# Key blocks of an RWKV-7 layer: one place per block for the small products, stages a whole block apart, and receptance inputs mixed from gate block 2 on

## The chip, the cores and the metric

The kernel runs on one core of one Trainium2 chip. The metric is the device time of one execution in microseconds (us); three executions of the kernel before gave a median of 1172.75 us. In the views of the profile PE is TensorE, PEld its weight loads, DVE VectorE, ACT ScalarE, POOL GpSimd and SP SyncE, which issues most of the transfers.

## The reference, cut to what matters

A sequence of 256 tokens with 2048 channels goes through one RWKV-7 layer and one sparse-attention layer, and everything is float32. Only the first part of the first layer matters here:

```python
xx = token_shift(u) - u
mixed = u[None] + xx[None] * mu[:, None, None, :]
rkvz = jnp.einsum('nbtd,nde->nbte', mixed[:4], w_rkvz)   # four 2048 x 2048 products
w_log = -jax.nn.softplus(-(w0 + jnp.tanh(xw @ w1) @ w2)) - 0.5
decay = jnp.exp(-jnp.exp(w_log.astype(jnp.float32)))
a = jax.nn.sigmoid(a0 + (xa @ a1) @ a2)
kk = heads(k * k_k).astype(jnp.float32)
kk = kk / jnp.maximum(jnp.sqrt(jnp.sum(kk * kk, axis=-1, keepdims=True)), 1e-12)
k = k * (1.0 + (a - 1.0) * k_a)
o = wkv7_scan(rh, heads(decay), kh, vh, -kk, kk * ah.astype(jnp.float32))
```

r, k, v and z are the receptance, key, value and gate projections. The scan over time is done in four chunks of 64 tokens, for which the kernel needs, per head and chunk, the product of the decayed `-kk` with the decayed keys, and the inverse of a triangular matrix built from it.

## The kernel before, in words

**Weights and inputs.** Every float32 product is made of three matmuls: high part by high part, high by low, low by high. A weight *piece* (128 x 512 numbers) is loaded by SP into a ring of 5 raw buffers (`wraw`, L177, two pieces to a buffer here), its high part is made by ACT (`whi`, L211) and its low part by DVE (`wlo`, L190), into rings of 5 buffers each. So DVE runs at most some four pieces ahead of PE. The mixed inputs (`mx`) are made per 128 channels by `mix` (L436): DVE computes `mtmp` (L433), ACT the high part (L426), DVE the low part (L427).

**The order of the projections.** v comes first, then gate block z0 (512 columns), the sixteen key blocks k0 to k15 (128 columns each, four pieces), gate blocks z1, z2 and z3 (sixteen pieces each), and then the receptance, whose products run among the steps of the scan (first line L1321). Counting the pieces from the start, k0 begins at piece 89, z1 takes pieces 153 to 168, z2 169 to 184, z3 185 to 200.

**A key block** (`phase_k`, L760) has 16 steps of three matmuls (L595 to L597). Between the steps stand small products that prepare the scan, and each hands on to DVE, ACT and POOL:

- `k_open(j)` (L678): two matmuls (L688, L689), then tanh on ACT, a running sum on DVE (`cum`, L695), exponentials on ACT, a memset on POOL (`sp`, L696) and a product on POOL (`an`, L702). It takes the next of three `sp` buffers.
- `k_square(j)` (L704), at the end of the block: ACT squares and copies the key, DVE scales it (`f`, L709).
- `k_norm(j)` (L711): the sums of squares (L715), then DVE (`sst`, L718), a power on POOL (`rnt`, L719) and a copy on ACT (`rnx`, L721).
- `k_turn(j)` (L724): transposes `rnx` (L728); DVE makes `nk` (L733) and a part of `sp` (L734), ACT another (L735), POOL the four products of `sp` (L739); SP stores `sp` (`spd`, L740).
- `k_close(j)` (L742): eight small matmuls that read `sp` (L749, each two instructions in the trace, as L688 and L689 are), two copies on ACT (`abs`, L752 and L753), three stores by SP (`abd`, L756).

In block j, after step 2, come `k_open(j)`, `k_turn(j-2)` and `k_norm(j-1)`, and after step 12 `k_close(j-2)`. `phase_z1` (L780) does the rest for the last two blocks, after steps 0, 2, 5 and 8. Half of the results of `k_close` go into a bank that `k_norm` and `k_turn` use too (`rn`).

**The inverse.** `inverse_ops(b)` (L796) inverts the triangular matrices of eight key blocks at a time, b = 0 after `k_close(7)`, b = 1 after `k_close(15)`. It loads them by SP (`invA`, L808 to L812) and then runs some 80 small operations, nearly all on DVE (L806), in chain. What of b = 1 is not yet written when the scan begins is dealt into the scan.

**What sets the order.** From k0 to z1 PE runs its instructions as the program writes them (L952). The other engines are put in order by a scheduler that works with modelled times, and then each runs its list strictly in that order: an instruction that waits holds up everything behind it on its engine. Background generators (`mixgen`, L547, and `stage_t`, L881) write the mixed inputs and the operations of the inverse among the steps, paced by pauses in modelled nanoseconds.

Of the kernel before, what the change touches and what calls it, by code (L numbers as in the profile page):

```python
# [12 lines left out]
AF = mybir.ActivationFunctionType  # L13
# [4 lines left out]
T, D, NK = 256, 2048, 16  # L18
# [50 lines left out]
HS, HSK = 300, 4  # L69
W1D, CXG = 5, 1  # L70
KPO = 3
KP, ZP = (2, 12), (0, 2, 5, 8)
AUX = {2: ("B0",), 3: ("G",), 4: ("B1",), 5: ("Y",), 7: ("A0",), 8: ("A1",), 9: ("T",)}
AUXL = {2: ("B0",), 3: ("G",), 4: ("B1",), 5: ("Y",), 8: ("T",), 9: ("A0",), 10: ("A1",)}
OPEN = (32, "G", "B0", "B1", 3, "Y", 3, "A0", 2, "A1", 8)
# [14 lines left out]
THB = 0  # L90
APOOL = 3
PRI = dict(chPE=0, chE=100, srPE=0, srE=0, skPE=0, skE=0, stE=0, atPE=1000, atE=0, cpPE=0, w=0, mx=0)
DV, DW, DK, DZ, DT, DL, DRM = 2000.0, 1000.0, 1400.0, 1200.0, 1000.0, 8000.0, 3000.0


class Sched:
# [128 lines left out]
def hybrid_kernel(ctx: ExitStack, tc: tile.TileContext, a: dict, out: bass.AP):  # L225
    nc = tc.nc
    V, S, G, PE = nc.vector, nc.scalar, nc.gpsimd, nc.tensor
# [35 lines left out]
    def accp(name="acc"):  # L263
        n = turn.get(name, 0)
        turn[name] = n + 1
        b = role[name]
        return psum.tile([128, 512], F32, name=f"bank{b[n % len(b)]}", bufs=1)
# [77 lines left out]
    phase_done = set()  # L345
# [90 lines left out]
    def mix(nm, k):  # L436
        split_into(mixed_in(nm, k), nm, k)
# [109 lines left out]
    def mixgen():  # L547
        for names in (("w", "a"), ("z",), ("k",), ("r",)):
            for k in range(NK):
                for nm in names:  # L550
                    if not ring_free(nm):
                        yield lambda: ring_free(nm)
                    if nm in "wa":
                        while ("v", k) not in mixed:
                            yield 300.0
                    mix(nm, k)
                    yield {"w": DW, "a": DW, "k": DK, "z": DZ, "r": DRM}[nm]
        phase_done.add("mixed")
# [115 lines left out]
    c3 = lambda x: x.rearrange("p (c t) -> p c t", c=NCH)  # L674
# [3 lines left out]
    def k_open(j):  # L678
        tmp = lambda name, bufs=2: kph.tile([128, T], F32, name=name, bufs=bufs)
        k = KST[j] = {}  # L680
        if j < 2:
            k["abs"] = tmp("abs")
        k["sp"] = sp = kph.tile([128, SPW], F32, name="sp", bufs=3)
        k["pp"] = pp = sp[:, 512:512 + NCH * (CH + 1)].rearrange("p (c t) -> p c t", c=NCH)
        w2t = w2[j // 2]
        sc = (j % 2) * 128
        la = accp("la")
        PE.matmul(la[:, :256], w2t[:, 0, sc:sc + 128], hw, start=True, stop=True)  # L688
        PE.matmul(la[:, 256:], w2t[:, 1, sc:sc + 128], ha, start=True, stop=True)  # L689
        sch.t += 720  # L690
        thw, tha, cum = tmp("thw"), tmp("tha"), tmp("cum")
        S.activation(thw, la[:, :256], AF.Tanh, scale=0.5, bias=W0H[:, j:j + 1])
        S.activation(tha, la[:, 256:], AF.Tanh, scale=0.5, bias=A0H[:, j:j + 1])
        S.activation(thw, thw, AF.Copy, scale=0.5, bias=0.5)
        V.tensor_tensor_scan(cum, C("rst"), thw, 0.0, op0=OP.mult, op1=OP.add)  # L695
        G.memset(pp[:, :, 0:1], 1.0)  # L696
        S.activation(pp[:, :, 1:], c3(cum), AF.Exp, scale=-DECAY)
        k["pinv"], k["an"], k["f"] = [tmp(n, 3) for n in ("pinv", "an", "f")]
        S.activation(k["pinv"], cum, AF.Exp, scale=DECAY)
        S.activation(k["an"], tha, AF.Copy, scale=-0.5, bias=-0.5)  # L700
        S.activation(k["f"], tha, AF.Identity, scale=KAH[:, j:j + 1], bias=KAM[:, j:j + 1])
        G.tensor_tensor(k["an"], k["an"], k["pinv"], op=OP.mult)  # L702
# [8 lines left out]
    def k_norm(j):  # L711
        k = KST[j]
        k["rn"] = rn = accp("rn")
        for tt in range(2):
            PE.matmul(rn[:, 256 + 2 * tt:258 + 2 * tt], k["sqk"][:, tt * 128:(tt + 1) * 128], C("bo"), start=True, stop=True)  # L715
        sch.t += 410
        sst, rnt = [kph.tile([128, 2, 2], F32, name=n, bufs=2) for n in ("sst", "rnt")]
        V.tensor_scalar(sst, rn[:, 256:260].rearrange("p (a b) -> p a b", a=2), 1e-24, None, op0=OP.max)  # L718
        G.tensor_tensor(rnt, sst, half[:, 0:4].rearrange("p (a b) -> p a b", a=2), op=OP.pow)  # L719
        k["rnx"] = kph.tile([128, T], F32, name="rnx", bufs=2)  # L720
        S.activation(k["rnx"].rearrange("p (a b n) -> p a b n", a=2, b=2),  # L721
                     rnt[:, :, :, None].to_broadcast([128, 2, 2, 64]), AF.Copy)

    def k_turn(j):  # L724
        k = KST[j]
        rn, sp, an, f, pinv = [k[n] for n in ("rn", "sp", "an", "f", "pinv")]
        for tt in range(2):
            PE.transpose(rn[:, tt * 128:(tt + 1) * 128], k["rnx"][:, tt * 128:(tt + 1) * 128], ident)  # L728
        sch.t += 215
        k["BK"] = BK = sp[:, 0:512].rearrange("p (c x t) -> p c x t", c=NCH, x=2)  # L730
        k["at"] = at = sp[:, SPW - 256:]
        nk = kph.tile([128, T], F32, name="nk", bufs=2)
        V.scalar_tensor_tensor(nk, k["ksb"], KKN[:, j:j + 1], rn[:, :256], op0=OP.mult, op1=OP.mult)  # L733
        V.tensor_tensor(c3(at), c3(nk), k["pp"][:, :, 0:CH], op=OP.mult)  # L734
        S.activation(sp[:, SPW - 512:SPW - 256], f, AF.Copy, scale=RK[:, j:j + 1])  # L735
        for x, y, o in ((f, pinv, 1), (nk, an, 0)):
            for h in range(2):
                r = slice(64 * h, 64 * h + 64)
                G.tensor_tensor(BK[r, :, h ^ o, :], c3(x)[r], c3(y)[r], op=OP.mult)  # L739
        nc.sync.dma_start(spd[j], sp)  # L740

    def k_close(j):  # L742
        k = KST.pop(j)
        ab = accp("ab")
        for c in range(NCH):
            for h in range(2):
                r, o = [slice(64 * i, 64 * i + 64) for i in (h, h ^ (c % 2))]
                pc = (ab, k["rn"])[c % 2][o, (384 if c % 2 else 0) + c // 2 * 64:]
                PE.matmul(pc[:, :64], c3(k["at"])[r, c, :], k["BK"][r, c, h, :], start=True, stop=True)  # L749
        sch.t += 500  # L750
        abs_ = k["abs"] if j < 2 else kph.tile([128, T], F32, name="abs", bufs=2)
        S.activation(abs_[:, 0:128], ab[:, 0:128], AF.Copy)  # L752
        S.activation(abs_[:, 128:256], k["rn"][:, 384:512], AF.Copy)  # L753
        for c, src, dst in ((0, 0, 0), (2, 0, 64), (2, 64, 0)):
            n = 64 if c else 128
            nc.sync.dma_start(abd[j, c:c + 2, :, dst:dst + n].rearrange("c k p s -> p (c k) s"),  # L756
                              abs_[src:src + n, 64 * c:64 * c + 128].rearrange("p (n s) -> p n s", s=32))
        a1done.add(j)

    def phase_k(j):  # L760
        if j % 2 == 0 and j + 2 < NK:
            load_pair(j // 2 + 1)
        o = accp("acc")[:, :T]
        for q in range(4):
            for s, cost in enumerate(cols_step(o, "k", q)):
                yield cost
                n = 4 * q + s
                if n == KP[0]:
                    k_open(j)
                    if j > 1:  # L770
                        k_turn(j - 2)
                    if j:
                        k_norm(j - 1)
                elif n == KP[1] and j > 1:
                    k_close(j - 2)
            if j == NK - 1:
                used.update(("k", k) for k in range(4 * q, 4 * q + 4))
        k_square(j, o)

    def phase_z1():  # L780
        turn["acc"] += 4
        ps = two()
        for k in range(NK):
            yield from rows_step(ps, "z", k, W.get(), 512)
            if k == ZP[0]:
                k_turn(NK - 2)
                k_norm(NK - 1)
            elif k == ZP[1]:
                k_close(NK - 2)
            elif k == ZP[2]:  # L790
                k_turn(NK - 1)
            elif k == ZP[3]:
                k_close(NK - 1)
        close_z(1, ps, [kph.tile([128, 512], F32, name="zth", bufs=2) for _ in range(2)], nc.sync)

    def inverse_ops(b):  # L796
# [6 lines left out]
        PE, V, S, G = Ranked(nc.tensor, "stE"), Ranked(nc.vector, "stE"), Ranked(nc.scalar, "stE"), Ranked(nc.gpsimd, "stE")  # L803

        def op(eng, n, fn, *args, pause=0.0, **kw):
            ops.append((eng, n, lambda: fn(*args, **kw), pause))  # L806
# [6 lines left out]

        flat = Tm.rearrange("p a b -> p (a b)")
        fa = A.rearrange("p a b -> p (a b)")
        op("Q", 0, load, pause=10000.0 if b else 6000.0)
        op("G" if b else "V", 1024, (G if b else V).memset, Tm, 0.0, pause=500.0)
        op("V", 32, V.memset, flat[:, 0::33], 1.0)
        op("V", 16, V.tensor_copy, flat[:, 32::66], fa[:, 32::66], pause=1000.0)
# [6 lines left out]
        for lv in (2, 4):  # L826
            n = 32 // (2 * lv)
# [1200 lines left out]
```

## Time and profile before

| | |
|---|---|
| median of three runs (lowest, highest) | 1172.75 us (1171.05, 1173.44) |
| the profiled execution's own time | 1173.38 us |
| its span, first to last instruction | 1171.5 us |
| PE busy | 1117.0 us, 95% |
| DVE busy | 874.9 us, 75% |
| ACT busy | 715.8 us, 61% |
| POOL busy | 365.9 us, 31% |
| bytes moved | 225.35 MB, mean 192 GB/s |

The profiled execution lies 0.63 us above the median, and 1.9 us of its time lie outside the span. Times in the views count from the span's start. In a row of the timeline stand the start, the duration (both us), the engine, the line, the operation and in brackets how long the engine had been idle before it and what it waited for. Rows of the grouped view hold the sum of the busy time and the mean duration in ns. In the view by windows the number in brackets counts instructions, and PEclk is the TensorE clock granted, 1.00 being full. Some matmul records are missing from a trace, so that counts can be a few short.

### The profile page before, as it was taken

Reading aid. Unit: us, or ns where it says so; the run is one execution under the profiler, and the core shown is the slowest. Engines: PE = TensorE matmul, PEld = TensorE weight load, DVE = VectorE, ACT = ScalarE, POOL = GpSimd, SP = SyncE. Lnnn points to the kernel's source line nnn. Section 1 sums busy time; section 2 is a strip of 40 time slices with the busy share of each in tenths; the row PEclk is TensorE's granted clock in tenths of the full one; section 3 lists DMA queues with packets and bytes.
Section 4 is the critical chain, followed back from the end, with each engine's and each line's share of the span. In section 5 each row is a group of like instructions: output and inputs, shape, how many; then the busy total and the mean of one; then the engine's idle time right before and its main releaser. Section 6 shows DMA issues by size and latency. Waiting matters only on the chain.

```text
span 1171.5 us, 24532 instructions
## 1 busy us (share of the span) xinstructions
PE 1117.0 (95%) x8880; PEld 948.3 (81%) x8880; DVE 874.9 (75%) x1807; ACT 715.8 (61%) x1696; POOL 365.9 (31%) x460
## 2 busy tenths in 40 slices
PE   8999989987789999899999999999999999999997
PEld 7788889976578777687778888788889989888786
DVE  6999866689855888587665878585576888988564
ACT  5667677767446455455564766575556676666553
POOL 1400046745441553555100001010233334452211
PEclk9999999999799999899999999999999999999999
DMA  6558967876698966867446867676665553748553
GB/s 221 171 182 244 255 189 214 226 202 171 192 251 233 254 174 183 235 151 215 125 154 194 254 195 238 209 252 192 171 176 148 144 141 95 190 117 273 172 184 108
DMA packets 239033, 225.35 MB, mean 192 GB/s; under 512 B 58053, under 2 KB 185333, under 8 KB 238912
## 3 DMA queue, kind: packets, MB, share of 16 engines
q1 hardware_dynamic: 233632, 217.17, 63.3%
q0 software_dynamic: 5280, 6.61, 2.3%
q8 instruction: 70, 1.15, 0.4%
q14 instruction: 51, 0.42, 0.1%
HBM read 200.48 MB, written 23.10 MB: 191 GB/s over the span
## 4 chain that ended last, share of the span: by engine, by line
PE 73%; DVE 10%; DMA 5%; POOL 5%; issue 4%; ACT 2%; SPq 0%; POOLq 0%; ACTq 0%; DVEq 0%
PE bank L577 11%; PE bank L579 11%; PE bank L576 11%; PE bank L1321 5%; PE bank L601 4%; DVE wlo L190 3%; POOL sp L739 3%; PE bank L602 2%; PE bank L1324 2%; PE bank L241 2%; PE bank L595 2%; PE bank L596 2%; PE bank L597 2%; PE pair L1343 1%; DMA spd<-sp 1%
## 5 line engine op out<-in xcount | busy, mean ns | idle before, releaser
L190 DVE TENSOR_TENSOR wlo<-wraw,whi 128x512 fp32r<-128x512 f32 (+2 forms) x616 | 448.7, 743 | 177.0 <-ACT whi L211 166.5
L211 ACT ACTIVATE whi<-wraw 128x512 fp32r<-128x512 f32 (+2 forms) x664 | 401.8, 620 | 243.3 <-PE bank L579 95.8
L577 PE MATMUL bank<-wlo,mx 128*128 128x512 f32 (+3 forms) x576 | 218.7, 381 | 5.5 <-DVE wlo L190 4.6
L579 PE MATMUL bank<-whi,mx 128*128 128x512 f32 (+3 forms) x576 | 216.9, 379 | 0.0
L576 PE MATMUL bank<-whi,mx 128*128 128x512 f32 (+3 forms) x576 | 190.9, 381 | 1.2 <-ACT whi L211 0.5
L577 PEld LDWEIGHTS bank<-wlo,mx 128*128 128x128 f32 x576 | 110.1, 191 | 24.5 <-DVE wlo L190 6.6
L576 PEld LDWEIGHTS bank<-whi,mx 128*128 128x128 f32 x576 | 109.3, 191 | 19.6 <-ACT mx L1909 1.2
L579 PEld LDWEIGHTS bank<-whi,mx 128*128 128x128 f32 x576 | 110.0, 191 | 17.0 <-POOL mx L1910 0.4
L1321 PE MATMUL bank<-mx,whi 128*128 128x512 f32 x256 | 102.7, 432 | 0.0
L190 POOL TENSOR_TENSOR wlo<-wraw,whi 128x512 fp32r<-128x512 f32 (+2 forms) x48 | 63.8, 1331 | 110.0 <-ACT whi L211 89.2
L601 PE MATMUL bank<-mx,whi 128*128 128x512 f32 x240 | 86.7, 397 | 0.0
L595 PE MATMUL bank<-mx,whi 128*128 128x256 f32 (+1 forms) x288 | 86.1, 299 | 0.3 <-ACT mx L426 0.3
L596 PE MATMUL bank<-mx,whi 128*128 128x256 f32 (+1 forms) x288 | 83.1, 289 | 0.0
L597 PE MATMUL bank<-mx,wlo 128*128 128x256 f32 (+1 forms) x288 | 83.0, 288 | 0.0
L577 PE MATMUL bank<-wlo,kvh 128*128 128x512 f32 x192 | 76.9, 401 | 0.0
L579 PE MATMUL bank<-whi,kvl 128*128 128x512 f32 x192 | 76.1, 396 | 0.0
L1324 PE MATMUL bank<-mx,wlo 128*128 128x256 f32 x256 | 71.0, 285 | 0.0
L602 PE MATMUL bank<-mx,wlo 128*128 128x256 f32 x256 | 70.5, 285 | 0.2 <-DVE wlo L190 0.2
L576 PE MATMUL bank<-whi,kvh 128*128 128x512 f32 x192 | 67.3, 395 | 0.0
L426 ACT ACTIVATE mx<-mtmp 128x256 fp32r<-128x256 f32 x96 | 38.6, 412 | 31.0 <-DVE mtmp L433 30.9
L595 PEld LDWEIGHTS bank<-mx,whi 128*128 128x128 f32 (+1 forms) x288 | 55.6, 193 | 2.3 <-ACT mx L426 0.7
L1321 PEld LDWEIGHTS bank<-mx,whi 128*128 128x128 f32 x256 | 48.2, 190 | 10.6
(344 smaller groups left out, 2326.9 us busy)
## 6 DMA issues: line engine op xcount, KB each, us to landing
wraw<-in_a_w_rkvz_dram SPq DMA_DIRECT2D x128, 512.0 KB, 5.3
wraw<-in_kv_w_dram SPq DMA_DIRECT2D x48, 512.0 KB, 4.5
wraw<-in_b_w_in_dram SPq DMA_DIRECT2D x40, 512.0 KB, 4.2
wraw<-in_a_w_o_dram SPq DMA_DIRECT2D x32, 512.0 KB, 4.6
wraw<-in_b_w_o_dram SPq DMA_DIRECT2D x32, 512.0 KB, 4.4
spd<-sp SPq DMA_DIRECT2D x16, 642.0 KB, 4.3
wraw<-in_b_w_in_dram SPq DMA_DIRECT2D x24, 384.0 KB, 3.3
spl<-spd SPq DMA_DIRECT2D x14, 642.0 KB, 6.4
```

Source lines behind the costliest of these rows:

```text
L190: eng.tensor_tensor(lv, src, hv.bitcast(F32), op=OP.subtract)
L211: self.nc.scalar.activation(hv, src, AF.Copy)
L576: PE.matmul(o, mh[:, ts], wh[:, 0, :], start=k == ends[0], stop=False)
L577: PE.matmul(o, mh[:, ts], wl[:, 0, :], start=False, stop=False)
L579: PE.matmul(o, ml[:, ts], wh[:, 0, :], start=False, stop=k == ends[1])
L595: PE.matmul(o, wh[:, s, :], mh, start=k == 0 and first, stop=False, **kw)
L596: PE.matmul(o, wh[:, s, :], ml, start=False, stop=False, **kw)
L597: PE.matmul(o, wl[:, s, :], mh, start=False, stop=k == NK - 1, **kw)
L601: PE.matmul(o, wh[:, s, :], joint[nm, k], start=k == 0, stop=False, **kw)
L602: PE.matmul(o[:, :T], wl[:, s, :], mh, start=False, stop=False, **kw)
L1321: both = lambda: PE.matmul(o, wh[:, s, :], joint["r", k], start=k == 0, stop=k == NK - 1)
L1324: PE.matmul(o[:, :T], wl[:, s, :], mixed["r", k][0], start=False, stop=False)
```

## The change

In a key block all small products now stand in one place, after step 3, in the order `k_close(j-3)`, `k_open(j)`, `k_turn(j-2)`, `k_norm(j-1)`. A block's `k_close` thus comes a whole block after its `k_turn`, where it came ten steps after it. In z1 the same order goes on after steps 0, 6 and 12. `k_close` writes to two banks of its own. The mixed inputs of the receptance are written after z1 instead of from the end of k15 on, with a shorter pause (2000 for 3000), and the pause after the load of the second inverse is shorter (8000 for 10000). The number of instructions of each kind stays.

```diff
-KP, ZP = (2, 12), (0, 2, 5, 8)
+KP, ZP = 3, (0, 6, 12)
...
-DV, DW, DK, DZ, DT, DL, DRM = 2000.0, 1000.0, 1400.0, 1200.0, 1000.0, 8000.0, 3000.0
+DV, DW, DK, DZ, DT, DL, DRM = 2000.0, 1000.0, 1400.0, 1200.0, 1000.0, 8000.0, 2000.0
...
+                    if nm == "r" and k == 0:
+                        yield lambda: "z1" in phase_done
                     mix(nm, k)
...
     def k_close(j):
         k = KST.pop(j)
-        ab = accp("ab")
+        ab, cd = accp("ab"), accp("ab")
...
-                pc = (ab, k["rn"])[c % 2][o, (384 if c % 2 else 0) + c // 2 * 64:]
-                PE.matmul(pc[:, :64], c3(k["at"])[r, c, :], k["BK"][r, c, h, :], start=True, stop=True)
+                PE.matmul((ab, cd)[c % 2][o, c // 2 * 64:c // 2 * 64 + 64], c3(k["at"])[r, c, :], k["BK"][r, c, h, :], start=True, stop=True)
...
-        S.activation(abs_[:, 128:256], k["rn"][:, 384:512], AF.Copy)
+        S.activation(abs_[:, 128:256], cd[:, 0:128], AF.Copy)
...
-                if n == KP[0]:
-                    k_open(j)
-                    if j > 1:
-                        k_turn(j - 2)
-                    if j:
-                        k_norm(j - 1)
-                elif n == KP[1] and j > 1:
-                    k_close(j - 2)
+                if n == KP:
+                    for lag, part in ((3, k_close), (0, k_open), (2, k_turn), (1, k_norm)):
+                        if j >= lag:
+                            part(j - lag)
...
-            if k == ZP[0]:
-                k_turn(NK - 2)
-                k_norm(NK - 1)
-            elif k == ZP[1]:
-                k_close(NK - 2)
-            elif k == ZP[2]:
-                k_turn(NK - 1)
-            elif k == ZP[3]:
-                k_close(NK - 1)
+            if k in ZP:
+                for lag, part in ((3, k_close), (2, k_turn), (1, k_norm)):
+                    j = NK + ZP.index(k) - lag
+                    if j < NK:
+                        part(j)
+        phase_done.add("z1")
...
-        op("Q", 0, load, pause=10000.0 if b else 6000.0)
+        op("Q", 0, load, pause=8000.0 if b else 6000.0)
```

Lines of the changed kernel differ by a few: L733 becomes L735, L739 L741, L749 L750, L806 L800.

PE, inside a key block: what stood before after step 2 (the closing products stood 30 matmuls further down, after step 12).

```order
L597 MATMUL bank_2765<-mx_1428,wlo 128x256
L688 MATMUL bank_2780<-hw,w2s 128x256
L689 MATMUL bank_2780<-ha,w2s 128x256
L728 MATMUL bank_2678<-cst,rnx 128x128 x2
L715 MATMUL bank_2810<-cst,t_2758 128x2 x2
L595 MATMUL bank_2765<-mx_1444,whi 128x256
```

PE, inside a key block of the changed kernel, after step 3:

```order
L599 MATMUL bank_2492<-mx_1444,wlo 128x256
L750 MATMUL bank_2509<-sp 64x64 x2
L750 MATMUL bank_2510<-sp 64x64 x2
L750 MATMUL bank_2509<-sp 64x64 x2
L750 MATMUL bank_2510<-sp 64x64 x2
L690 MATMUL bank_2526<-hw,w2s 128x256
L691 MATMUL bank_2526<-ha,w2s 128x256
L730 MATMUL bank_2423<-cst,rnx 128x128 x2
L717 MATMUL bank_2556<-cst,t_2485 128x2 x2
L597 MATMUL bank_2492<-mx_1467,whi 128x256
```

The closing products (L750, alternately to two banks; a row gathers several of them) now come ahead of the opening ones; the transposes and sums follow as before.

POOL, one key block, before: the memset of the next `sp` buffer stands ahead of all four products of L739.

```order
L696 MEMSET sp_3176 128x4
L739 TENSOR_TENSOR sp_3047<-f_3062,pinv_3060 64x4x64 x2
L739 TENSOR_TENSOR sp_2908<-nk_3198,an_2922 64x4x64 x2
L719 TENSOR_TENSOR rnt_3211<-sst_3210,half_108 128x4
L702 TENSOR_TENSOR an_3190<-an_3190,pinv_3189 128x256
```

POOL, one key block, in the changed kernel:

```order
L741 TENSOR_TENSOR sp_3188<-f_3203,pinv_3201 64x4x64 x2
L698 MEMSET sp_3325 128x4
L741 TENSOR_TENSOR sp_3051<-nk_3347,an_3065 64x4x64 x2
L721 TENSOR_TENSOR rnt_3360<-sst_3359,half_108 128x4
L704 TENSOR_TENSOR an_3339<-an_3339,pinv_3338 128x256
```

The memset now stands between the two pairs; the first pair belongs to the block that turns next, the second to the one that has just been turned.

DVE, end of z1 and start of z2 in the changed kernel (the first row is the 167th `wlo`; `mtmp` and `mx` are the receptance's mixed inputs, L800 the inverse):

```order
L190 TENSOR_TENSOR wlo<-wraw,whi 128x512
L427 TENSOR_TENSOR mx_4474<-mtmp,mx_4474 128x256
L433 SCALAR_TENSOR_TENSOR mtmp<-xx,prm,xn 128x256
L190 TENSOR_TENSOR wlo<-wraw,whi 128x512
L800 TENSOR_REDUCE invT<-invX 128x8x8
L190 TENSOR_TENSOR wlo<-wraw,whi 128x512
L427 TENSOR_TENSOR mx_4519<-mtmp,mx_4519 128x256
L433 SCALAR_TENSOR_TENSOR mtmp<-xx,prm,xn 128x256
L190 TENSOR_TENSOR wlo<-wraw,whi 128x512
L427 TENSOR_TENSOR mx_4541<-mtmp,mx_4541 128x256
L800 TENSOR_TENSOR invX<-invT,invM 128x512
L190 TENSOR_TENSOR wlo<-wraw,whi 128x512
```

DVE, the end of the first inverse before:

```order
L733 SCALAR_TENSOR_TENSOR nk<-ksb,par,bank_3894 128x256
L190 TENSOR_TENSOR wlo<-wraw,whi 128x512
L806 TENSOR_TENSOR invX<-invT,invM 128x1024
L190 TENSOR_TENSOR wlo<-wraw,whi 128x512
L734 TENSOR_TENSOR sp<-nk,sp 128x256
L190 TENSOR_TENSOR wlo<-wraw,whi 128x512
L806 TENSOR_REDUCE invT<-invX 128x8x8
L190 TENSOR_TENSOR wlo<-wraw,whi 128x512 x5
```

Before, the last row of the first inverse stands after the 165th `wlo`; now it stands after the 180th, and seven of its rows after the 168th. Its first row (a copy from `invA`) stood after the 134th `wlo` and stands now after the 138th. Of the sixteen `mx` rows of the receptance, all sixteen stood ahead of the 163rd `wlo`; now twelve stand ahead of the 168th, and the last after the 173rd. The first row of the second inverse stood after the 173rd and stands after the 194th.

## The prediction

> **What bounds the kernel now.** I read the view by windows first, cut where the code changes stage: the key blocks until the first inverse begins (157.6 to 237.0), the rest of them and of z1 while it runs, the end of z1, and z2 with z3 until the receptance begins at 377.4. The last three rows look at short stretches behind waits.
>
> ```profile
> core 0: us, PE busy (x) PEld busy (x) DVE busy (x) ACT busy (x) POOL busy (x), PEclk, DMA share, GB/s
> 157.60:237.00 79.40, 74.65 (x670) 70.55 (x669) 51.34 (x79) 59.02 (x155) 51.58 (x62) 0.98 0.76 208
> 237.00:316.00 79.00, 59.95 (x442) 52.92 (x441) 76.34 (x163) 47.86 (x121) 38.00 (x42) 0.91 0.64 179
> 316.00:328.20 12.20, 12.20 (x53) 9.84 (x54) 4.02 (x7) 4.62 (x9) 8.79 (x17) 0.74 0.94 309
> 328.20:377.40 49.20, 46.13 (x197) 37.71 (x196) 28.44 (x62) 25.25 (x44) 10.85 (x21) 0.97 0.90 237
> ...
> 176.00:179.00 3.00, 3.00 (x15) 2.98 (x15) 1.07 (x2) 2.20 (x7) 0.91 (x3) 0.51 0.65 182
> 301.00:304.00 3.00, 2.95 (x23) 2.41 (x24) 3.00 (x8) 1.05 (x4) 0.00 (x0) 0.63 0.79 231
> 257.60:260.60 3.00, 3.00 (x34) 2.90 (x35) 2.90 (x8) 1.94 (x6) 1.79 (x2) 1.00 0.78 219
> ```
>
> Two bounds follow each other. In the first window PE is busy for 94% and DVE for 65%: PE sets the pace, and what it loses are waits. In the second DVE is busy for 76.34 of 79.00 us and PE for 59.95: DVE sets the pace. From 328.2 on PE leads again, with DVE at 58%. The waits of PE from 150 to 380 have two rows that matter, both for the closing products:
>
> ```profile
> PE bank L749 <- POOL sp L739: 14.7, 12, 3.4
> PE bank L749 <- DVE sp L734: 9.1, 3, 5.2
> ```
>
> Their places and the edges of the stages stand in PE's timeline:
>
> ```profile
> 157.63 0.60 PE L688 MATMUL bank<-hw,w2s 96*128 96x256 f32 x2
> ...
> 165.50 0.59 PE L688 MATMUL bank<-hw,w2s 96*128 96x256 f32 x2
> ...
> 173.51 0.32 PE L749 MATMUL bank<-sp 64*64 64x64 f32 x2 [2.73 <-POOL sp L739]
> ...
> 225.39 0.75 PE L749 MATMUL bank<-sp 64*64 64x64 f32 x16
> ...
> 236.72 0.59 PE L688 MATMUL bank<-hw,w2s 96*128 96x256 f32 x2
> ...
> 256.79 0.32 PE L749 MATMUL bank<-sp 64*64 64x64 f32 x2 [1.05 <-POOL sp L739]
> ...
> 301.05 0.46 PE L749 MATMUL bank<-sp 64*64 64x64 f32 x16 [2.78 <-DVE sp L734]
> ...
> 315.19 0.33 PE L749 MATMUL bank<-sp 64*64 64x64 f32 x2 [3.40 <-POOL sp L739]
> ...
> 339.38 0.80 PE L577 MATMUL bank<-wlo,mx 128*128 128x512 f32 x1 [3.07 <-DVE wlo L190]
> ...
> 377.38 0.39 PE L1321 MATMUL bank<-mx,whi 128*128 128x512 f32 x1
> ```
>
> A block without a stall takes 157.63 to 165.50, 7.87 us. The eight from k3 (165.50) to k11 (236.72) took 71.22 where eight times 7.87 is 62.96, so 8.3 us were lost, to such waits and to the slow clock behind them (0.51 in the window at 176). DVE's timeline shows the second bound:
>
> ```profile
> 238.94 0.18 DVE L806 COPY invT<-invA 128x16 f32<-128x16 f32 x1 [5.51 <-DMA invA<-abd]
> ...
> 310.82 0.47 DVE L733 SCALAR_TENSOR_TENSOR nk<-ksb,par,bank 128x256 f32<-128x256 f32 x1
> ...
> 320.30 0.69 DVE L190 TENSOR_TENSOR wlo<-wraw,whi 128x512 fp32r<-128x512 f32 x1 [3.81 <-ACT whi L211]
> ...
> 322.87 0.69 DVE L190 TENSOR_TENSOR wlo<-wraw,whi 128x512 fp32r<-128x512 f32 x1 [1.88 <-ACT whi L211]
> ...
> 338.08 0.18 DVE L806 COPY invT<-invA 128x16 f32<-128x16 f32 x1 [5.95 <-DMA invA<-abd]
> 338.17 0.18 DVE L806 TENSOR_TENSOR invM<-invA,invT 128x32 f32<-128x32 f32 x1
> ```
>
> The first inverse begins at 238.94, after DVE had waited 5.51 us for its load. From there DVE works on, nearly without a gap, until `nk` of block 15 at 310.82. The last `wlo` of z1 (the 168th) is the row at 322.87. So z1 ends when DVE has done everything that stands between the inverse's first row and the 168th `wlo`.
>
> **The change part by part.** I count from the order of the changed kernel what stands on DVE between those two rows, and price it from the rows grouped by form of 140 to 365:
>
> ```profile
> L190 DVE TENSOR_TENSOR wlo<-wraw,whi 128x512 fp32r<-128x512 f32 x106 | 81.7, 778 | 40.8 <-ACT whi L211 39.1 <-PE bank L688 1.5
> ...
> L806 DVE TENSOR_TENSOR invX<-invT,invM 128x1024 f32<-128x1024 f32 x2 | 2.4, 1212 | 0.0
> ...
> L806 DVE TENSOR_REDUCE invT<-invX 128x64 f32<-128x512 f32 x2 | 1.3, 672 | 0.0
> ...
> L427 DVE TENSOR_TENSOR mx<-mtmp,mx 128x256 fp32r<-128x256 f32 x16 | 8.1, 514 | 0.0
> ...
> L433 DVE SCALAR_TENSOR_TENSOR mtmp<-xx,prm,xn 128x256 f32<-128x256 f32 x13 | 6.9, 540 | 0.0
> ```
>
> A row begins about 0.08 before the one ahead has ended (338.08 plus 0.18 is 338.26, the next begins at 338.17), so each is worth its duration less 0.08.
>
> *The inverse's start.* Its load reads the stores of `k_close(7)`. That ran at 225.39 in block 9, and the copy came 13.55 later. Now `k_close(7)` stands after step 3 of block 10. Block 10 would begin seven blocks after 165.50, at 220.6 if nothing stalls, and its closing products come 0.36 later; I add 0.5 for a leftover stall, which makes 221.5. With the same 13.55 the copy comes at 235.0, 3.9 us earlier. The closing products themselves no longer wait: the order puts a whole block, 7.87 us, between the turn of a block and its close, and at a distance of ten steps they waited 2.73 at 173.51 and 1.05 at 256.79. So nearly all of the 8.3 goes, but only 3.9 counts, since DVE then waits for the load. The second bank costs nothing that I can find: the two copies on ACT remain, and the banks come free a block later. Bounds: 0 if the load lands as much later, 8.3 if it waits for nothing.
>
> *Less work on DVE before z1 ends.* Four `wlo` now stand ahead of the copy (138 for 134): 4 x 0.70, the middle between 0.69 alone less 0.08 and the mean of 0.78, makes 2.8. Seven rows of the inverse stand behind the 168th `wlo`: four of 1024 elements, 4 x 1.13, and three of 512, 3 x 0.60 (0.672 rounded, less 0.08), make 6.3. Four `mx` stand behind it, 4 x 0.43 makes 1.7, and two `mtmp`, 2 x 0.46 makes 0.9. Sum: 11.7. Nothing comes in their place. The bound below is 0, if the rows wait on something else; above it is 13, at full durations.
>
> The mean `wlo` took 778 ns, against 690 in the quiet rows at 320.30 and 322.87; POOL works beside the slower ones. [...]
>
> *The waits at z1's end.* DVE waited 3.81 + 1.88 = 5.7 between `nk` of block 15 and the 168th `wlo`, because ACT and the weight ring stood behind PE, and PE behind the close at 315.19. Now the last close comes six steps after its turn, so the 5.7 go. Bounds: 0 and 5.7; I take the upper, since what is late next is `wlo` itself.
>
> *The tail.* The 168th `wlo` ended at 323.56, z1 at about 328.2, 4.6 later, as PE had to catch up at a clock of 0.74. A z piece takes 1.36, by two rows of the chain of waits:
>
> ```profile
> 348.98 0.45 PE bank L576 x2
> ...
> 350.34 0.45 PE bank L576 x2
> ```
>
> If PE has been waiting for `wlo`, the tail is 1.4 at least. I take 2.3, another 2.3 less.
>
> Sum at z1's end: 3.9 + 11.7 + 5.7 + 2.3 = 23.6 earlier.
>
> *z2 and z3.* They took 49.2 (328.2 to 377.4), of which 32 x 1.36 = 43.5 is the pace. PE waited 3.07 at 339.38, since DVE stood 5.95 at 338.08 for the second inverse's load with the next `wlo` behind it. In the changed order that first row stands after the 194th `wlo` instead of the 173rd, and its load is asked for well ahead. So the wait of 3.07 goes. But the 6.3 + 1.7 = 8.0 us of DVE work displaced from z1 falls here, at the moment when DVE has no lead: of it I charge 3.3 in place of 5.7, and z2 with z3 take 46.8: 2.4 gained. Bounds: 43.5, all hidden in DVE's idle 20.8 us, and 51.5, all in PE's way (2.3 lost).
>
> *The clock.* One gap will remain: at z1's step 0 the turn of block 14 waits for `rnx`, made only after DVE and POOL have worked off the norm. The rows at 301.05 and in its window show a gap of 2.78 and then 0.63 for 3 us: 1.1 us lost. I charge 1.0. Behind the 1.05 at 256.79, the window at 257.6 shows 1.00. [...]
>
> From 377.4 on the orders of PE, DVE and ACT agree row by row, save 60 rows of the inverse instead of 62 in the scan: nothing.
>
> In all 23.6 + 2.4 - 1.0 = 25.0. On the profiled execution's own 1173.38 that gives 1148.4; the median is 0.63 lower, and the forecast is 1172.75 - 25.0 = 1147.8.
>
> **The rivals.**
>
> *Slower: one place per block makes a loop through POOL.* Everything now turns over once a block: POOL's memset of an `sp` buffer waits for the store of its earlier contents, behind it stand the pair `nk`, `rnt`, and then ACT's `rnx`, without which the next turn holds PE, and each later matmul, up.
>
> ```profile
> L739 POOL TENSOR_TENSOR sp<-nk,an 64x256 f32<-64x256 f32 x32 | 33.9, 1058 | 14.7 <-DVE nk L733 11.9 <-DVE sst L718 0.6
> ...
> L721 ACT ACTIVATE rnx<-rnt 128x256 f32<-128x256 f32 x16 | 6.6, 414 | 15.9 <-POOL rnt L719 15.9
> ...
> L719 POOL TENSOR_TENSOR rnt<-sst,half 128x4 f32<-128x4 f32 x16 | 19.6, 1223 | 1.3
> ```
> ```profile
> 162.98 7.62 DMA spd<-sp
> ```
> ```profile
> spd<-sp SPq DMA_DIRECT2D x16, 642.0 KB, 4.3
> ```
>
> From a block's opening at T: about 0.9 for the opening products, 0.4 for the turn, 0.5 for `nk` and 2 x 1.06 for POOL's pair bring the store to T + 3.9. With the longest landing seen, 7.62, the memset comes at T + 11.5, that is 3.6 into the next block; the pair, `rnt` and `rnx` add 2.1 + 1.2 + 0.4, so `rnx` is there at 7.3, and it is needed at 7.87 + 0.7 + 0.9 = 9.4. The median landing of 4.3 leaves 5.4. It decides from landings of about 9.7 on. If each of ten blocks then lost a wait like that at 173.51 with the clock behind it, 2.73 + 3 x 0.49 = 4.2, that would be 42 lost against 25 gained: about 1190. Against it: no landing seen is so long. Chance 0.08.
>
> *Half of it.* DVE stays the bound, but its displaced rows and the receptance's mixing cost PE in z2 all that they save in z1 (z2 and z3 at 51.5, 4.7 more than forecast), and the load is as late as before (the 3.9 gone): 25.0 - 8.6 = 16.4; if the waits at z1's end stay too, 10.7. That is 1156 to 1162. For it speaks that DMA is busy for 0.90 to 0.94 of the time at the end of z1 and after. Chance 0.20.
>
> *All of it.* PE runs at its own pace throughout. Its idle time in the four windows is 4.75 + 19.05 + 0 + 3.07 = 26.9, and the clock cost, on PE's busy time, 74.65 x 0.02 + 59.95 x 0.09 + 12.20 x 0.26 + 46.13 x 0.03 = 11.5, so up to 38: 1135 to 1141. DVE's load in the second window speaks against it. Chance 0.06.
>
> *Nothing.* The receptance begins earlier, but the scan's opening then waits for what the inverses give, and the end stays. The last row of the first inverse stands only 12 `wlo` behind z1's end, with the receptance yet to come: chance 0.04, 1172.
>
> **How the numbers follow.** The forecast has 0.62, with a range of its own of 1141 to 1155 (its bounds on the start, on z2 and on the tail, each some 2 to 4 us, seldom all on one side). The range of 8 in 10 takes it in, two thirds of the half case and a little of the full one: 1139 to 1161. A measurement of this kernel can tell about 0.2%, 2.3 us, from no change. Faster by more: 0.62 + 0.20 + 0.06 = 0.88; within it: 0.04; slower: 0.08.
>
> **What would show each step right or wrong.** Right: no wait at the closing products longer than 1 us before z1; the opening of k11 at about 229; the copy at about 235 after a wait of DVE of some 3 us for its load; z1's end at about 304; the first matmul of the receptance at about 352; its distance to the end unchanged at 794. Wrong would be: the transposes of `k_turn` waiting for `rnx` in block after block; the copy's wait as long as before with PE no earlier; a `wlo` group that stays at 778 ns and more with PE waiting for it through z2; or a first receptance matmul 25 us earlier and an end that has not moved.

## The result, and the profile after

The changed kernel takes 1142.82 us (median of five runs, 1142.49 to 1144.25), the kernel before 1171.94 (five runs, 1169.30 to 1173.44): a ratio of 0.9755, 95% interval 0.974 to 0.9771, so some 29 us faster where 25 were forecast. The profiled executions have spans of 1171.5 and 1140.4, 31.1 apart; that of before lies 1.4 above the median of its five runs, that of after 0.3 below.

The view by windows of the changed kernel, cut at the same events as before (up to the first inverse's first row; from there to the end of z1; z2 with z3; the receptance and the rest), and one short stretch:

```profile
core 0: us, PE busy (x) PEld busy (x) DVE busy (x) ACT busy (x) POOL busy (x), PEclk, DMA share, GB/s
157.30:233.30 76.00, 76.00 (x708) 72.66 (x707) 52.85 (x84) 62.84 (x160) 53.22 (x65) 1.00 0.85 242
233.30:303.70 70.40, 63.08 (x455) 53.73 (x454) 69.69 (x153) 47.21 (x119) 40.32 (x44) 0.93 0.66 197
303.70:348.40 44.70, 44.46 (x196) 36.19 (x195) 36.11 (x76) 26.73 (x47) 19.11 (x32) 1.00 0.98 293
348.40:1140.40 792.00, 772.54 (x6749) 649.01 (x6747) 576.52 (x1194) 471.09 (x1133) 234.74 (x287) 0.99 0.63 185
...
277.20:283.70 6.50, 6.50 (x32) 5.00 (x33) 6.50 (x10) 2.90 (x9) 2.63 (x3) 0.50 0.65 203
```

In the first window PE is never idle and at full clock. In the second VectorE (DVE) is busy for 69.69 of 70.40 us. In the third PE is busy for 44.46 of 44.70. What PE still waits for, from 150 to 380:

```profile
PE bank L578 <- ACT ksb L710: 5.0, 1, 5.0
PE bank L717 <- ACT t L709: 1.3, 3, 0.4
PE bank L750 <- POOL sp L741: 0.7, 1, 0.7
```

The closing products waited 23.8 us before (14.7 on POOL's `sp`, 9.1 on DVE's); now 0.7. In their place one wait of 5.0 is left. Its row, and the edges of the stages, in PE's timeline:

```profile
157.31 0.59 PE L690 MATMUL bank<-hw,w2s 96*128 96x256 f32 x2
...
219.80 0.46 PE L750 MATMUL bank<-sp 64*64 64x64 f32 x16
...
236.56 0.46 PE L750 MATMUL bank<-sp 64*64 64x64 f32 x14 [0.68 <-POOL sp L741]
...
277.20 0.80 PE L578 MATMUL bank<-whi,mx 128*128 128x512 f32 x1 [4.98 <-ACT ksb L710]
...
348.39 0.39 PE L1315 MATMUL bank<-mx,whi 128*128 128x512 f32 x1
```

And in DVE's timeline the first rows of the two inverses, with the last `wlo` of z1 between them; ACT's first row on z1's result marks that stage's end:

```profile
233.32 0.19 DVE L800 COPY invT<-invA 128x16 f32<-128x16 f32 x1 [3.80 <-DMA invA<-abd]
...
300.37 0.68 DVE L190 TENSOR_TENSOR wlo<-wraw,whi 128x512 fp32r<-128x512 f32 x1
...
335.42 0.19 DVE L800 COPY invT<-invA 128x16 f32<-128x16 f32 x1 [0.43 <-DMA invA<-abd]
```
```profile
303.85 1.24 ACT L647 ACTIVATE zth<-bank 128x512 f32<-128x512 f32 x2
```

The same events in both traces (before, z1's end by that mark is 328.42):

| stage, us | before | after | gained | forecast |
|---|---|---|---|---|
| first row of the first inverse, at | 238.94 | 233.32 | 5.6 | 3.9 |
| from there to the end of z1's last `wlo` | 84.6 | 67.7 | 16.9 | 17.4 |
| from there to z1's end | 4.9 | 2.8 | 2.1 | 2.3, less 1.0 for the clock at z1's start |
| z2 and z3, to the receptance | 49.0 | 44.5 | 4.4 | 2.4 |
| receptance, scan and the rest | 794.1 | 792.0 | 2.1 | 0 |

### The profile page after: what moved, and what is told of

It is laid out like the page before. It is cut to its first block, busy times and chain, and to the rows that moved or that the text cites. A ratio compares the mean times of both kernels' runs of the same rounds, so it can differ in the third digit from the quotient of the medians.

```text
span 1140.4 us, 24521 instructions
## 1 busy us (share of the span) xinstructions
PE 1106.3 (97%) x8880; PEld 939.2 (82%) x8880; DVE 873.3 (77%) x1807; ACT 716.3 (63%) x1696; POOL 368.9 (32%) x460
## 4 chain that ended last, share of the span: by engine, by line
PE 73%; DVE 11%; DMA 6%; issue 4%; POOL 3%; ACT 2%; SPq 0%; ACTq 0%; POOLq 0%; DVEq 0%
PE bank L579 12%; PE bank L581 12%; PE bank L578 12%; PE bank L603 5%; PE bank L1315 4%; DVE wlo L190 3%; PE bank L604 3%; PE bank L241 2%; PE bank L1318 2%; PE bank L597 2%; PE bank L598 2%; PE bank L599 2%; PE pair L1337 2%; DVE mtmp L433 1%; PE pair L1339 1%
## 5 line engine op out<-in xcount | busy, mean ns | idle before, releaser
L597 PE MATMUL bank<-mx,whi 128*128 128x256 f32 (+1 forms) x288 | 83.7, 291 | 0.3 <-ACT mx L426 0.3
L598 PE MATMUL bank<-mx,whi 128*128 128x256 f32 (+1 forms) x288 | 82.1, 285 | 0.0
```

What stands on the lines that cost most here:

```text
L597: PE.matmul(o, wh[:, s, :], mh, start=k == 0 and first, stop=False, **kw)
L598: PE.matmul(o, wh[:, s, :], ml, start=False, stop=False, **kw)
```

## The experiments

The theory of the prediction: from the first inverse's first row on, what stands on DVE up to the last `wlo` of z1 sets z1's end; the places of the small products change that list, and the block between a turn and its close takes PE's waits away. Rivals: the gain comes from the receptance's inputs; or PE's waits were all, and DVE's list counts for nothing. Each kernel ran beside the kernel before on the same chip (medians there 1170.65 to 1171.6), so ratios are compared.

**The places alone, and the rest alone.** The gate and the pause of the receptance's inputs turned out to move no instruction: without them, the order of the changed kernel is the same row for row on every engine, and twelve of the sixteen mixed inputs still stand ahead of z1's last `wlo`. Only the pause of the second inverse's load moves rows. The first kernel takes all of that away, the second has only that.

```diff
-DV, DW, DK, DZ, DT, DL, DRM = 2000.0, 1000.0, 1400.0, 1200.0, 1000.0, 8000.0, 2000.0
+DV, DW, DK, DZ, DT, DL, DRM = 2000.0, 1000.0, 1400.0, 1200.0, 1000.0, 8000.0, 3000.0
...
-                    if nm == "r" and k == 0:
-                        yield lambda: "z1" in phase_done
...
-        op("Q", 0, load, pause=8000.0 if b else 6000.0)
+        op("Q", 0, load, pause=10000.0 if b else 6000.0)
```

> Only the places of the small products and the second bank are changed; the receptance's inputs and both pauses are as before. Theory (the end of z1 is set by what stands on VectorE between the first inverse's first row and the last wlo of z1, and only the places change that list): nearly the whole gain stays, 1142 to 1145 us, and the receptance begins at 348 to 350. Rival (a good part of the gain comes from the receptance inputs written later): 1155 to 1168.

> Only the receptance's inputs (written after z1, pause 2000) and the pause of the second inverse's load are changed; places and banks are as before. Theory: the rows on VectorE ahead of z1's end stand as before, so 1169 to 1173 us, no more than 3 below the kernel before, and the waits at the closing products stay. Rival: 10 or more below the kernel before.

Measured: the places alone 1147.64 us, 0.9807 (0.9785 to 0.9828); the inputs and pauses alone 1171.51 us, 1.0006 (0.9991 to 1.002). The rival is out. But the first lies above the 1142 to 1145 expected and 0.4 to 0.5% above the changed kernel (0.9755 above, 0.9772 when measured again below, where the intervals touch), and it starts the receptance at 348.9, only 0.5 later. It loses the rest in the scan. PE's timeline shows one wait there that the changed kernel lacks:

```profile
441.36 1.12 PE L1188 MATMUL pair<-cst,O 64*64 64x64 f32 x32 [2.25 <-DVE O L1176]
```

and DVE's timeline what stood ahead of `O`:

```profile
434.60 0.67 DVE L798 TENSOR_REDUCE invT<-invX 128x32 f32<-128x512 f32 x1
```

It is the last reduction of the second inverse, and on ACT, too, two copies of its result stand ahead of the rows that make `O`. In the changed kernel the reduction stands at 428.72. With the long pause, nine more rows of the second inverse on DVE (69 for 60) are left for the scan. Aligned on the same matmuls, the two traces stand 0.8 apart the other way at 431 and 3.3 this way at 463. So the pause is worth about 4 us, though alone, in the kernel before, it is worth nothing.

**A later start of the inverse, with no wait.** The closing products keep their three blocks, but stand nine steps later.

```diff
+                if n == 12 and j > 2:
+                    k_close(j - 3)
                 if n == KP:
-                    for lag, part in ((3, k_close), (0, k_open), (2, k_turn), (1, k_norm)):
+                    for lag, part in ((0, k_open), (2, k_turn), (1, k_norm)):
```

> The changed kernel, but the closing products of block j-3 stand after step 12 of block j instead of after step 3: a block and nine steps behind their turn. They still wait for nothing, but the first inverse can begin only nine steps, 3.3 us, later. Theory (VectorE's list from that first row sets z1's end): the first row comes at about 236.5 instead of 233.3, z1 ends and the receptance begins 2 to 3.5 later, 1144.5 to 1146.5 us. Rival (the gain is PE's waits at the closing products alone): the same time as the changed kernel, 1142 to 1143.5.

Measured 1143.6 us, 0.9768 (0.9748 to 0.9789): no difference from the changed kernel, as the rival had it, so this run alone does not speak against the rival. Its profiled execution, 1139.67 us, lies 3.9 below the median. The first row came where it was expected:

```profile
236.50 0.18 DVE L802 COPY invT<-invA 128x16 f32<-128x16 f32 x1 [3.43 <-DMA invA<-abd]
```

But the last `wlo` of z1 ended at 300.29, not later than the 301.05 of the changed kernel. I had priced the start and taken the list behind it as given. Counted row by row, that list took 63.8 us for 67.7: one `wlo` and four of the key blocks' rows stand ahead of the first row, where DVE has time while it waits for the load, and the inverse's rows ran 1.4 shorter, while two more `mx` and one more `mtmp` stand in the list. A start and the list behind it can't be priced apart.

**Receptance inputs really late.** Each reads a copy of the mixing factors that depends on the turn of block 15.

```diff
+    def late_mu(src):
+        m = ph1.tile([128, NK], F32, name="mur", bufs=1)
+        V.scalar_tensor_tensor(m, src, 0.0, MU[0], op0=OP.mult, op1=OP.add)
+        MUR.append(m)
...
-        mu = MU[{"r": 0, "k": 1, "v": 2, "z": 3, "w": 4, "a": 5}[nm]]
+        mu = MUR[0] if nm == "r" else MU[{"r": 0, "k": 1, "v": 2, "z": 3, "w": 4, "a": 5}[nm]]
...
+                        if part is k_turn and j == NK - 1:
+                            late_mu(KST[j]["BK"].rearrange("p a b c -> p (a b c)")[:, 0:NK])
```

> The changed kernel, but the receptance's mixed inputs really come late: each reads a copy of the mixing factors that is made from a product of block 15's turn, so none of them stands ahead of the last wlo of z1 (twelve did). The seven rows of the first inverse that stood behind z1 stand ahead of it instead, and the second inverse's first row stands after the 175th wlo. Theory: VectorE has 12 mx and as many mtmp less, 11 us, and 7 inverse rows more, 6.3, ahead of z1's end, and ScalarE's copy of block 15's key no longer stands behind a mixing (PE waited 4.98 there): z1 ends 4 to 7 earlier; z2 and z3 give back up to 5, as all mixing falls there and the second inverse's first row may wait for its load again: 1137 to 1144 us, most likely 1140. Rival (that wait and the mixing are off the path): the same as the changed kernel or slower, 1143 to 1147.

Measured 1151.88 us, 0.9834 (0.9812 to 0.9857): some 8 us slower than the changed kernel, against my expectation. PE's timeline and its view by windows:

```profile
277.55 0.79 PE L585 MATMUL bank<-whi,mx 128*128 128x512 f32 x1 [5.01 <-ACT ksb L717]
...
320.95 0.79 PE L586 MATMUL bank<-wlo,mx 128*128 128x512 f32 x1 [3.95 <-DVE wlo L190]
```
```profile
275.00:305.60 30.60, 28.05 (x153) 22.26 (x154) 28.16 (x48) 18.00 (x39) 8.78 (x11) 0.83 0.66 205
305.60:357.00 51.40, 45.99 (x190) 36.92 (x189) 36.34 (x88) 27.73 (x53) 18.64 (x35) 0.93 0.95 256
```

Two things took the gain. DVE's list up to z1's last `wlo` is as long as before the edit, 67.8 us: its twelve `mx` and eight of its eleven `mtmp` are gone from it, 10.0 us, but seven more rows of the inverse (6.0), longer small rows (1.9) and 2.4 of waits fill the place. And the second inverse's first row moved from behind the 194th `wlo` to behind the 175th, where DVE waits 5.62 for its load at 319.69 and PE behind it 3.95: the same wait that the kernel before had at 339.38. By ACT's mark z1 ends at 304.89 (the windows above are cut at 305.60), 1.0 later than in the changed kernel, and z2 and z3 take 52.1 for 44.5. The wait for `ksb` did not go either. In the changed kernel ACT waits ahead of `ksb` for two `mtmp` of DVE (2.22 and 0.45); here the mixing is gone from there, and ACT waits instead for DVE's `cum` and then 0.43 for POOL's `rnt`:

```profile
274.25 0.42 ACT L706 ACTIVATE sp<-cum 128x256 f32<-128x256 f32 x1 [1.98 <-DVE cum L704]
```

In both kernels ACT is held up there mostly by DVE, for 2.67 us and for 1.98.

**More work on DVE, in three kernels.** The low part of eight pieces is computed twice, 8 x 0.69 = 5.5 us: pieces 158 to 165, in z1, in the changed kernel and in the kernel before, and pieces 105 to 112, in key blocks 4 and 5, in the changed kernel.

```diff
         self.due.append((lv, src, hv, eng))
+        if 157 <= self.split < 165:
+            self.due.append((lv, src, hv, eng))
```

> The changed kernel with the low part of eight weight pieces in z1 (158 to 165) computed twice on VectorE: 8 x 0.69 = 5.5 us more on its list ahead of z1's end, and nothing else. The theory of the prediction (VectorE's list up to the last wlo sets z1's end): z1 ends 4.5 to 5.5 later, 1147.5 to 1148.5 us. The theory that the first experiments left standing (PE sets z1 itself, and VectorE's lateness reaches PE only through the chain of the small products): 0 to 2 more, 1143 to 1145.

> The kernel before with the same eight low parts computed twice. Both theories expect a loss here, since the wlo stand ahead of the nk and sp of the last two blocks, for which PE waits at the closing products: 3 to 7 us, 1174 to 1178. If it stays within 1 us of the kernel before, VectorE was not the bound of z1 there either, and the gain came from somewhere else.

The third kernel has 104 and 112 for 157 and 165.

> The changed kernel with the low part of eight pieces of key blocks 4 and 5 (105 to 112) computed twice: 5.5 us more on VectorE while it has a third of its time free, ahead of the first inverse. Theory (VectorE is the bound only from the first inverse's first row to the end of z1): 0 to 1 more, 1142 to 1144. Rival (any work on VectorE counts, through the clock or through the small products): 3 to 10 more.

Measured: in z1 of the changed kernel 1158.66 us, 0.99 (0.9879 to 0.9921), some 15 us more than the changed kernel; in z1 of the kernel before 1174.11 us, 1.003 (1.0019 to 1.0041), 3.5 more; in the key blocks of the changed kernel 1145.02 us, 0.9788 (0.977 to 0.9807), 1.7 more than the changed kernel beside it, with intervals that overlap, between what the theory and the rival expected and nearer to the theory (its first inverse starts 1.9 later, at 235.23). PE's waits in the first of them, and its windows of z1 and of z2 with z3:

```profile
PE bank L581 <- DVE wlo L190: 9.9, 7, 2.1
PE bank L580 <- ACT ksb L712: 5.0, 1, 5.0
```
```profile
277.00:314.30 37.30, 30.39 (x156) 22.28 (x156) 37.27 (x67) 18.19 (x43) 8.06 (x8) 0.90 0.58 174
314.30:363.70 49.40, 45.25 (x186) 35.04 (x186) 31.29 (x67) 25.25 (x45) 19.74 (x37) 0.97 0.94 261
```

The dose lands on the path in full: DVE has not a tenth of a us idle in z1, its list is 6.1 longer (73.8), and PE, which waited for no `wlo` in the changed kernel, now waits for seven. What I had not expected is the multiple: the receptance begins 15.4 later (363.76 for 348.39). PE's last matmul of z1 comes 8.6 later (312.66 for 304.06; ACT's row at 314.29, which marks the end of the window, is late here, as ACT copies a result of the inverse first), and the other 6.8 fall in z2 and z3. They are not the dose on the list alone. The edit also moved the second inverse's first row, from behind the `wlo` of piece 194 to behind that of piece 183, where DVE waits for its load and PE then 1.90 for the next `wlo`, at 338.02:

```profile
336.73 0.18 DVE L802 COPY invT<-invA 128x16 f32<-128x16 f32 x1 [3.32 <-DMA invA<-abd]
```

In the kernel before, the same dose was taken up by idle time: the waits of DVE on the way to z1's last `wlo` shrank from 5.69 to 0.68 and the list stayed at 84.6. The 3.5 that it costs there cannot be placed, since its profiled execution, which lies 1.7 below the median, reaches the receptance at 377.53 (377.38 before).

**z1 without the wait at its start.** It accumulates in banks that block 15 does not use, and its small products stand after steps 4, 9 and 14.

```diff
-KP, ZP = 3, (0, 6, 12)
+KP, ZP = 3, (4, 9, 14)
...
-        turn["acc"] += 4
```

> The changed kernel, but z1 accumulates in the two banks that block 15 does not use, and its small products stand after steps 4, 9 and 14 instead of 0, 6 and 12, so that z1 can begin while VectorE, GpSimd and ScalarE still work off the last blocks. The theory that PE is the bound of z1 and lost 4.98 us of wait at its first step and some 3 by the clock behind it: 5 to 8 us less, 1135 to 1138. The theory of the prediction (VectorE's list is the bound): no more than 1 less, 1142 to 1144.

Measured 1147.44 us, 0.9805 (0.9785 to 0.9824), slower than the changed kernel. PE's timeline and a window:

```profile
279.02 0.50 PE L579 MATMUL bank<-wlo,mx 128*128 128x512 f32 x1 [3.00 <-DVE wlo L190]
...
293.84 0.46 PE L750 MATMUL bank<-sp 64*64 64x64 f32 x16 [1.45 <-DVE sp L736]
...
352.20 0.63 PE L1314 MATMUL bank<-mx,whi 128*128 128x512 f32 x1 [2.57 <-DVE vt L649]
```
```profile
271.00:304.30 33.30, 27.41 (x169) 21.30 (x168) 33.30 (x60) 21.18 (x51) 15.88 (x16) 1.00 0.62 190
279.00:282.50 3.50, 2.86 (x11) 2.08 (x12) 3.50 (x6) 2.44 (x6) 0.74 (x1) 1.00 0.51 194
```

The wait for `ksb` is gone, the clock stays at 1.00, PE works on at z1 from 272.9, where it had stood until 277.2, and z1 ends at 304.3, no earlier than without the edit (303.85): PE now waits for DVE, 3.00 and 0.61 for `wlo` and 1.45 for `sp`. This is the clearest sign that DVE's list sets the end of z1. The loss comes later: the receptance's first bank is now one that z3 has just used, and PE waits 2.57 for it at 352.20.

**One bank.** Half of the closing products' results go back into the norm's bank.

```diff
-        ab, cd = accp("ab"), accp("ab")
+        ab, cd = accp("ab"), k["rn"]
```

> The changed kernel, but half of the closing products' results go into the bank that the norm uses, as before the change. That bank is needed again by the norm of two blocks later, which now stands right behind the closing products, so PE must wait until ScalarE has copied it out. Theory that the second bank is needed for the new place: 1 to 2.5 us of wait in each of 13 blocks, 1155 to 1175 us. Rival (the copy is done by the time the transposes are over): 1142 to 1145.

Measured 1146.59 us, 0.9802 (0.9781 to 0.9823): about 4 us for the bank, far less than the theory expected and a little more than the rival did. PE waits for the copy, but only three times, where ACT's list is late; the first, of 3.38, in block 12:

```profile
PE bank L717 <- ACT abs L754: 4.8, 3, 3.4
```

**The distance undone.** Close nine steps behind its turn, in two banks, all else as changed; and the changed kernel once more beside it.

```diff
+                if n == 12 and j > 1:
+                    k_close(j - 2)
                 if n == KP:
-                    for lag, part in ((3, k_close), (0, k_open), (2, k_turn), (1, k_norm)):
+                    for lag, part in ((0, k_open), (2, k_turn), (1, k_norm)):
...
+            if k in (3, 9):
+                k_close(NK - 2 + k // 9)
             if k in ZP:
-                for lag, part in ((3, k_close), (2, k_turn), (1, k_norm)):
+                for lag, part in ((2, k_turn), (1, k_norm)):
```

> The changed kernel with the distance alone undone: the closing products of block j-2 stand after step 12 of block j, nine steps behind their turn (and in z1 after steps 3 and 9, three steps behind it), in two banks of their own; everything else as changed. Theory that the block between turn and close is what takes PE's waits away: waits of 1 to 5 us at the closing products come back, 10 to 25 us in all, and 1158 to 1172 us. Rival (putting the opening, the turn and the norm one step later, or the second bank, is what counts): 1142 to 1150.

> The changed kernel once more, beside the other two on the same chip: 1141 to 1144 us, ratio 0.974 to 0.977.

Measured: 1168.81 us, 0.9983 (0.9972 to 0.9994), and the changed kernel 1143.3 us, 0.9772 (0.9752 to 0.9791). The distance is nearly the whole gain, some 25 of 27 us here. PE's waits are back:

```profile
PE bank L750 <- POOL sp L741: 10.7, 12, 2.4
PE bank L750 <- DVE sp L736: 7.7, 3, 3.5
PE bank L579 <- DVE wlo L190: 6.2, 1, 6.2
```

So is DVE's long list: 80.6 us from the first row to z1's last `wlo`, with 34 `wlo`, 71 rows of the inverse and all 16 `mx`, as in the kernel before, and the second inverse's first row behind the 173rd `wlo`, with a wait of 8.43 for its load. That kernel reaches the receptance at 373.38, 25.0 later than the changed one: 1.0 of it lies ahead of the inverse's first row, 12.9 in the list (11.0 in more or longer rows, 1.9 in waits of DVE), 3.0 from the last `wlo` to z1's end and 8.1 in z2 and z3.

## Why the prediction was right

The forecast of 1147.8 us was 5.0 too high. On the profiled executions the gain was 31.1 for 25.0, and the table above has the differences: 1.7 at the start, 0.5 less in the list, 0.2 less behind it, the 1.0 for the clock, 2.0 in z2 and z3, 2.1 in the rest.

**The bound.** Right. The list of DVE took 67.7 us where the prediction's working gives 84.6 - 11.7 - 5.7 = 67.2, z1 ended at 303.85 (the sum gives 328.2 - 23.6 = 304.6, or 305.6 with the clock's 1.0; the list of signs says about 304), and DVE's waits on the way fell from 5.69 to 0. That this list is the path, and not only busy, is shown by the dose (the list 6.1 longer, z1's last matmul 8.6 later) and by z1 without the wait at its start, which ended no earlier. In the kernel before it was not quite full: the same dose there disappeared into DVE's waits.

**The parts of the list.** Their sum was right and the parts less so. Counted to the next row's start, 7 rows of the inverse are worth 4.7 (6.3 forecast), 4 `wlo` 3.7 (2.8), 4 `mx` 2.5 (1.7); the two `mtmp` gave nothing, since those that are left ran longer (6.7 us for 11, where 13 took 6.0), and the small rows gave 1.0. Together 11.2, forecast 11.7.

**The start.** `k_close(7)` ran at 219.80 and the first row came 13.52 later, as the 13.55 of before had it. It came 1.7 earlier than forecast, since no stall was left at all and the closing products stand ahead of the opening ones; the opening of k11 came at 228.07 (forecast about 229). That DVE then waits for the load was right (3.80, forecast about 3).

**z2 and z3.** 44.5 for the 46.8 forecast: I charged 3.3 for the 8.0 us of work displaced there, and it cost 1.0 (43.5 is the pace). The wait of 3.07 is gone.

**The gap at z1's start.** The place was right, the cause was not, and the clock's 1.0 had no place in the sum. PE waited 4.98 there, for ACT's `ksb` of block 15 and not for `rnx`, and ran at 0.50 for the 6.5 us behind it. Yet DVE held z1's end, so that neither cost anything: without them it came no earlier.

**The scan: nearly right by luck.** "From 377.4 on ... nothing": the term of the pause was never priced. The changed kernel runs this stretch 2.1 faster (792.0 for 794.1), of which up to 1.8 can be the distances of the two profiled executions from their medians. But without the shorter pause the stretch takes 797.1, 3.0 more than in the kernel before. So two terms of opposite sign were left out, the earlier receptance and the pause, and they nearly cancelled. The number of rows of the inverse left for the scan (60, 69 without the pause) was in the order to be read; what it costs depends on where the last one stands, and that the receptance's earlier start makes it matter was missed.

**The rivals.** The loop through POOL did not come: the one wait for `rnx` is of 0.2 us. The landing of `spd` got slower, 5.3 us in the median for 4.3, and stayed, with 6.3 at the longest, under the 9.7 from which it would decide. "All of it" is ruled out as a mechanism by DVE's 69.69 of 70.40, though the time came nearer to its range (1135 to 1141) than to 1147.8: outside that stretch PE did run at nearly its own pace. "Half" named the wrong place: the pieces that it saw given back in z2 appear where the second inverse moves forward, as with the late inputs.

**What stays open.** The distance changed two things at once, PE's waits and the order on DVE, and both come back together when it is undone. The longer list of that kernel, 11.0 of 12.9 us in rows and 1.9 in DVE's waits, speaks for the order, but no run changes one without the other. That the receptance's inputs are of no account as an edit is shown; why the scheduler packs more on DVE ahead of z1's end at the short distance was not tried.

## What to carry to other kernels

Price the list of the engine that never idles between two fixed events, not the waits of the others: the change in its length gave the end of the stage to within 1 us, while removing PE's wait at the start of z1 did not move that end. When such a list is shortened, count it again after every edit, since a scheduler fills the place: an edit that took 10 us off it ended up slower. And an edit that does nothing alone may be needed by another: price it with the other in place.

## What the runs showed of the hardware

TensorE's granted clock after a gap did not follow the gap's length alone. In the changed kernel, after 4.98 us without work, it was 0.50 for 6.5 us (277.20 to 283.70). In the kernel before it was 0.51 from 176.00 to 179.00, after waits of 2.73 and 0.81, and 0.63 from 301.00 to 304.00, around the end of a wait of 2.78. In the kernel without the wait for `ksb` it was 1.00 from 279.00 to 282.50, with a wait of 3.00 ending at 279.02. What else it went by, no run here shows.

A dose of 5.5 us on the engine that sets the pace cost some 15 us, since `wlo` came late in two stages and the second inverse moved forward into a wait for its load. PE stands idle for 6.9 + 4.2 = 11.1 us in the two windows of that kernel, and 9.9 of it are listed as waits for `wlo`, of which the changed kernel has none there.
